# Refilling the operands of the down product one by one, on GpSimd's DMA queue

## The chip, the cores and the metric

One core of a Trainium2 chip. The metric is the device time of one execution in microseconds (us), as the median of several runs. All engine times below are from one profiled execution of the kernel.

## What is computed

The reference is one layer of a decoder (sparse attention beside retention, then a feed-forward block, then a gated embedding) on 1024 prompt tokens and 8 sample tokens. The change touches the feed-forward block alone:

```python
hn = rms_norm(h, n2)
h = h + (jax.nn.silu(hn @ wg) * (hn @ wu)) @ wd      # D_MODEL 1024, D_FF 2816
```

All of it is float32. The kernel writes each operand as a sum of a rounded high part and a low part (`split`), and each product as three matmuls (`mm3`: high by high, high by low, low by high).

## The kernel before

**Tiling.** The 1032 tokens are cut into two halves (`p` = 0, 1) of two quarters (CE = 258 tokens each); the features run on the partitions. `D_FF` is walked in NF = 11 slabs `f` of 256 features. Gate, up and down are computed by a fast two-by-two scheme: instead of eight block products, seven, numbered 1 to 7. Each has a weight operand (a sum or difference of blocks of the weights) and an activation operand `x1` to `x7` (the same of blocks of the activations). Gate and up use them in the order `FAST` = 1, 6, 5, 2, 7, 4, 3, down in the order `DOWN` = 1, 5, 6, 3, 2, 4, 7.

**Gate and up** (`gate_up`, L1840; `fast_product`, L1702). For each slab and each half the seven products of the gate, then of the up weights, run on TensorE. `run` (L1735) interleaves two of them: the last two products (4 and 3) of one come behind the first two (1 and 6) of the next. Their partial sums lie in a tile `wst` (2 buffers, L1713), and `up` and `finish` leave the seven operands of the down product in `act`, which SyncE's DMA queue stores to `act_d` in HBM (L1864), since the operands of all slabs don't fit on the chip.

**Down** (`down`, L1927). The 11 slabs are taken in three parts, `PARTS` = slabs 0 to 2, 3 to 6, 7 to 10. In each part, for four column groups `mp` of the down weights, and in each for both halves `p`, the seven products of `kt` matmul triples run (3 triples in part 0, else 4) and are added into the result `h` (L1944 a copy on ScalarE, L1946 an add on VectorE). A product's sum lies in one of seven banks of PSUM, which come free with these adds.

**Fetching the operands** (`act_fetch`, L1877). The seven operands `x1` to `x7` of a half have one buffer each (`xtile`, L1751), the same that gate and up used. For each operand `act_fetch` loads two slabs at a time (258 KB), or the third slab alone (129 KB), into a raw tile, and `split` (L150) makes of it the high part by a cast on ScalarE (L152) and the low part by a subtraction on VectorE (L142, by L153). So each half and part takes 14 loads, and both halves 28. The raw tiles lie in two rings: `st` with three buffers, and `wst`, the ring of the gate and up products, with two; three loads of five use `st`. In the program `act_fetch` of part 0 stands ahead of the first `down` of each half (L1982), that of the next part behind the last `down` of the half (L1985).

**What sets the order.** The kernel is written with a scheduler: it puts each engine's instructions in an order of its own at compile time, by readiness in its own model of time and by the order of the program, and adds the semaphores. An instruction may so stand far ahead of its place in the program, where its buffer and its data allow; but once the order is made, each engine and each DMA queue works strictly in order, and an instruction that waits holds up all behind it. SyncE's queue issues the loads of `act_fetch`, those of the weights (`fast_weights`, L1675, L1680, tiles `wu`) and, in part 2, those of the residual (`h_d`, L1965, tiles `st`).

Of the kernel before, what the change touches and what calls it, by code (L numbers as in the profile page):

```python
# [10 lines left out]
F32 = mybir.dt.float32  # L11
# [109 lines left out]
def hybrid_kernel(tc, I, C, O):  # L121
# [1577 lines left out]
            operand(n, place[n])  # L1699
        return w  # L1700

    def fast_product(w, x, kt, take):  # L1702


        ba, bb, bc = bank("s", NS), bank("m", 2), bank("t", NT)

        def prod(b, n, first=True):

            for k in range(kt):
                mm3(b[:, :CE], w[n][0][:, k], w[n][1][:, k], x[n][0][:, k], x[n][1][:, k], first and k == 0, k == kt - 1,  # L1710
                    skip_group_check=not first)

        st = tl(pdr, [128, 2, CE], "wst", bufs=2)  # L1713
        s, t1, u3 = st[:, 0], st[:, 1], tl(pdr, [128, CE], "wu3")
        prod(ba, 1)
        A.copy(s, ba[:, :CE])
        prod(bb, 6)
        add(V, t1, bb[:, :CE], s)
        yield
        prod(bc, 5)  # L1720
        prod(ba, 2, False)
        take(0, 0, ba[:, :CE], None)
        prod(bb, 7, False)
        add(V, u3, bb[:, :CE], s)
        take(1, 1, bc[:, :CE], u3)
        yield
        prod(bb, 4, False)
        take(1, 0, bb[:, :CE], s)
        prod(bc, 3, False)
        take(0, 1, bc[:, :CE], t1)  # L1730
        yield
# [3 lines left out]
    def run(product, then=None):  # L1735

        if product:
            next(product)
        if going:
            g, f = going.pop()  # L1740
            next(g)
            if f:
                f()
        if product:
            next(product)
            going.append((product, then))
# [93 lines left out]
    def gate_up(w, f):  # L1840
# [27 lines left out]
        w = fast_weights(half_rows(I["w_up"], f * 256), 4, FAST)  # L1868
        for p in range(2):
            act = tl(pf, [128, 8, CE], "act", bufs=2)  # L1870
            run(fast_product(w, xs[p], 4, partial(up, p, act)), partial(finish, p, act))

    PARTS = ((0, 3), (3, 4), (7, 4))

    staged = [0]

    def act_fetch(p, f0, kt):  # L1877
        for n in DOWN:
            full[p][n] = xtile(p, n)
            xs[p][n] = hi, lo = tuple(x[:, :kt] for x in full[p][n])  # L1880
            for a in range(0, kt, 2):
                b = min(a + 2, kt)
                staged[0] += 1
                raw = tl(pdr, [128, 2, CE], *(("st", F32, 3), ("wst", F32, 2))[staged[0] % 5 % 2])[:, :b - a]
                SY.dma_start(raw, act_d[f0 + a:f0 + b, p, :, n - 1, :].rearrange("f p c -> p f c"))
                split(V, hi[:, a:b], lo[:, a:b], raw)

    w = fast_weights(half_rows(I["w_gate"], 0), 4, FAST)
    for g in (norm2(3), combine(1)):
# [37 lines left out]
    def down(n, kt, mp, p, w):  # L1927
# [6 lines left out]
        def prod(b, m, tag=None, bufs=None):  # L1934
            first = tag is not None
            if first:
                banks[b] = bank(tag, bufs)[:, :CE]
            for k in range(kt):
                mm3(banks[b], w[m][0][:, k], w[m][1][:, k], x[m][0][:, k], x[m][1][:, k], first and k == 0, k == kt - 1,
                    skip_group_check=not first)  # L1940

        def onto(c, b, fresh):
            if n == 0 and fresh:
# [33 lines left out]
    for n, (f0, kt) in enumerate(PARTS):  # L1977
        for mp in range(4):
            w = fast_weights(lambda half: wdv[half, :, f0:f0 + kt, mp * 256:(mp + 1) * 256], kt, DOWN)
            for p in range(2):  # L1980
                if n + mp == 0:
                    act_fetch(p, f0, kt)  # L1982
                down(n, kt, mp, p, w)
                if mp == 3 and n < 2:
                    act_fetch(p, *PARTS[n + 1])  # L1985
                elif mp == 3:
                    h_parts(p, range(8))
                    p_parts(p)

# [103 lines left out]
```

## Time and profile before

| | |
|---|---|
| median of 3 runs (lowest to highest) | 2144.17 us (2142.01 to 2145.64) |
| the profiled execution: its own time, its span | 2140.78 us, 2139.0 us |
| granted TensorE clock, mean | 0.986 of full speed |
| TensorE (PE) busy | 2045.0 us, 96% of the span |
| VectorE (DVE) busy | 1370.5 us, 64% |
| ScalarE (ACT) busy | 843.5 us, 39% |
| GpSimd (POOL) busy | 690.6 us, 32% |

The span runs from the first to the last instruction. PE is TensorE's matmul, PEld its weight load, DVE VectorE, ACT ScalarE, POOL GpSimd, SP SyncE; a q behind the name means its queue or sequencer. L152 is line 152 of the kernel. A releaser ("<-") is what ended an idle time, inferred from the semaphores; idle time of an engine that is not the bound costs nothing by itself. Gate and up end and the down product starts near 1764 us; down ends near 1995 us.

### The profile page before, as it was taken

The numbers are of one execution on the slowest core, as the hardware profiler recorded it, in microseconds if no ns is written. First come the engines' busy times: TensorE is split into PE (matmuls) and PEld (weight loads), VectorE is DVE, ScalarE is ACT, GpSimd is POOL, SyncE is SP. The second block draws the span as 40 slices with busy tenths as digits, with TensorE's granted clock in tenths as the row PEclk, the third lists the DMA queues.
The fourth block names the chain that finished last, engine by engine and source line by source line (L and its number), as shares of the span: only waits on it lengthen the run. The fifth ranks groups of instructions, "written<-read, shape, count | busy, mean of one in ns | idle before, by whom it ended". The sixth has DMA issues, their size and how long they took to land.

```text
span 2139.0 us, 38497 instructions
## 1 busy us (share of the span) xinstructions
PE 2045.0 (96%) x14824; PEld 1895.3 (89%) x14824; DVE 1370.5 (64%) x3135; ACT 843.5 (39%) x2091; POOL 690.6 (32%) x891
## 2 busy tenths in 40 slices
PE   7999999979999999999999898999999999999998
PEld 6998998867788886679999798999999999999998
DVE  4335145357778889677665458766666676878632
ACT  3331222236565654554444334323323335542321
POOL 1235334277777765757673033000000000000100
PEclk9999999989999999999999998999999999999999
DMA  6322223244334343644541731233233244553221
GB/s 225 136 73 74 75 69 87 59 125 134 106 117 123 109 126 109 204 145 143 158 153 44 218 95 47 94 122 107 79 112 102 85 141 147 179 154 125 91 74 50
DMA packets 186032, 246.77 MB, mean 115 GB/s; under 512 B 17252, under 2 KB 155144, under 8 KB 185656
## 3 DMA queue, kind: packets, MB, share of 16 engines
q1 hardware_dynamic: 160760, 160.40, 24.4%
q0 software_dynamic: 25088, 83.90, 12.6%
q8 instruction: 117, 1.92, 0.4%
q14 instruction: 67, 0.55, 0.1%
HBM read 204.09 MB, written 44.34 MB: 116 GB/s over the span
## 4 chain that ended last, share of the span: by engine, by line
PE 53%; DVE 6%; DMA 4%; ACT 1%; issue 1%; POOL 0%; DVEq 0%; ACTq 0%; POOLq 0%; SPq 0%
PE m L944 8%; PE s L157 5%; PE s L159 5%; PE s L158 5%; PE m L157 4%; PE m L159 4%; PE m L158 4%; PE t L157 3%; PE t L159 3%; PE t L158 3%; PE t L1144 2%; DMA wst<-act_d 2%; DVE x L142 1%; PE o L1133 1%; PE s L1268 1%
## 5 line engine op out<-in xcount | busy, mean ns | idle before, releaser
L944 PE MATMUL m<-seg,w1h 128*128 128x256 f32 x1024 | 296.3, 396 | 0.8 <-DVE scl L1048 0.8
L157 PE MATMUL s<-x,wu 128*128 128x258 f32 x872 | 248.9, 286 | 5.3 <-ACT x L152 3.3
L158 PE MATMUL s<-x,wu 128*128 128x258 f32 x872 | 248.5, 285 | 1.0 <-DVE x L142 0.9
L159 PE MATMUL s<-x,wu 128*128 128x258 f32 x872 | 247.8, 284 | 0.5 <-DVE wu L142 0.5
L142 POOL TENSOR_TENSOR x<-h,x 128x516 fp32r<-128x516 f32 x4 | 5.7, 1415 | 676.9 <-ACT x L152 676.9
L157 PE MATMUL m<-x,wu 128*128 128x258 f32 x768 | 218.9, 286 | 2.6 <-DVE h L148 1.5
L158 PE MATMUL m<-x,wu 128*128 128x258 f32 x768 | 218.1, 284 | 2.5 <-DVE x L142 2.5
L159 PE MATMUL m<-x,wu 128*128 128x258 f32 x768 | 217.9, 284 | 0.0
L944 PEld LDWEIGHTS m<-seg,w1h 128*128 128x128 f32 x1024 | 173.9, 194 | 20.8 <-issue 8.9
L152 ACT CAST wu<-wu 128x512 fp32r<-128x512 f32 (+2 forms) x178 | 109.6, 626 | 193.4 <-DVE wu L142 119.1
L953 DVE STREAM_TRANSPOSE seg<-raw 128x1024 f32<-128x1024 f32 x128 | 158.6, 1240 | 37.5 <-PE m L944 29.9
L157 PEld LDWEIGHTS s<-x,wu 128*128 128x128 f32 x872 | 165.8, 190 | 6.3 <-ACT x L152 3.7
L158 PEld LDWEIGHTS s<-x,wu 128*128 128x128 f32 x872 | 166.5, 191 | 1.6 <-DVE x L142 1.4
L159 PEld LDWEIGHTS s<-x,wu 128*128 128x128 f32 x872 | 166.4, 191 | 0.7 <-DVE wu L142 0.7
L142 DVE TENSOR_TENSOR wu<-wu,wu 128x512 fp32r<-128x512 f32 (+2 forms) x178 | 126.6, 715 | 61.7 <-ACT wu L152 60.1
L157 PE MATMUL t<-x,wu 128*128 128x258 f32 x528 | 150.8, 286 | 7.3 <-DVE h L148 4.9
L290 PE MATMUL g<-wh,xnh 128*128 128x256 f32 (+3 forms) x504 | 148.9, 296 | 2.5 <-ACT xnh L340 2.3
L158 PE MATMUL t<-x,wu 128*128 128x258 f32 x528 | 149.6, 283 | 0.5 <-DVE x L142 0.4
L159 PE MATMUL t<-x,wu 128*128 128x258 f32 x528 | 149.4, 283 | 0.3 <-DVE wu L142 0.3
L157 PEld LDWEIGHTS m<-x,wu 128*128 128x128 f32 x768 | 146.1, 190 | 4.0 <-issue 1.7
L158 PEld LDWEIGHTS m<-x,wu 128*128 128x128 f32 x768 | 146.6, 191 | 2.7 <-DVE x L142 2.7
L854 POOL DMA_INDIRECT raw<-in_cache_cmp_v_dram,cix x128 | 126.6, 989 | 66.9 <-issue 28.5
(474 smaller groups left out, 5977.8 us busy)
## 6 DMA issues: line engine op xcount, KB each, us to landing
act_d<-act SPq DMA_DIRECT2D x22, 903.0 KB
wr<-in_w_in_dram SPq DMA_DIRECT2D x12, 1024.0 KB
wu<-in_w_gate_dram SPq DMA_DIRECT2D x22, 512.0 KB
wu<-in_w_up_dram SPq DMA_DIRECT2D x22, 512.0 KB
st<-act_d SPq DMA_DIRECT2D x42, 258.0 KB
wu<-in_w_down_dram SPq DMA_DIRECT2D x16, 512.0 KB
wst<-act_d SPq DMA_DIRECT2D x28, 258.0 KB
mr<-mix_d SPq DMA_DIRECT2D x16, 258.0 KB
```

Source lines behind the costliest of these rows:

```text
L142: eng.tensor_tensor(out=out, in0=a, in1=b, op=ALU.subtract)
L152: A.copy(hi, src)
L157: P.matmul(out, wh, xh, start=first, stop=False, **kw)
L158: P.matmul(out, wh, xl, start=False, stop=False, **kw)
L159: P.matmul(out, wl, xh, start=False, stop=last, **kw)
L290: P.matmul(pt[:r, :n], xh, wh[:, k, :n], start=k == 0, stop=False)
L854: G.indirect_dma_start(out=raws[n, par][:, x, :], out_offset=None, in_=crow[kv], in_offset=bass.IndirectOffsetOnAxis(ap=cix[:, par, col:co ...
L944: P.matmul(out, w[:, k, :], x[:, k // 2 % 2, :, k % 2, :], start=first and k == 0, stop=k == 7, skip_group_check=not first)
L953: V.transpose(t.rearrange("p k (x d) -> p k x d", x=4), raws[n, par][:, :, s2 * 256:(s2 + 1) * 256].rearrange("p x (k d) -> p k x d", k=8))
L1133: P.matmul(u.po[:, :256], st[2], ph[:, x, :], start=u.done == 0, stop=False)
L1144: P.transpose(pt[:, (x * 2 + r) * 128:(x * 2 + r + 1) * 128], src[:, r, c0:c0 + 128], ident)
L1268: P.matmul(pt[x * 64:(x + 1) * 64, :256], qzb[:, b, :], kt[:, x * 256:(x + 1) * 256], start=True, stop=True)
```

## The change

Each operand is fetched right behind the last product that reads it: part 0 from within the last up product of each half (a new argument `used` of `fast_product`), the later parts from within `down` of the last column group. The loads are issued by GpSimd's queue in place of SyncE's. In part 0 they all use the ring `st`; the later parts use `st` and `wst` as before. The arithmetic is the same.

```diff
-    def fast_product(w, x, kt, take):
+    def fast_product(w, x, kt, take, used=None):
...
             for k in range(kt):
                 mm3(b[:, :CE], w[n][0][:, k], w[n][1][:, k], x[n][0][:, k], x[n][1][:, k], first and k == 0, k == kt - 1,
                     skip_group_check=not first)
+            if used:
+                used(n)
...
-            run(fast_product(w, xs[p], 4, partial(up, p, act)), partial(finish, p, act))
+            run(fast_product(w, xs[p], 4, partial(up, p, act), partial(act_fetch, p, 0) if f == NF - 1 else None),
+                partial(finish, p, act))
...
-    def act_fetch(p, f0, kt):
-        for n in DOWN:
-            full[p][n] = xtile(p, n)
-            xs[p][n] = hi, lo = tuple(x[:, :kt] for x in full[p][n])
-            for a in range(0, kt, 2):
-                b = min(a + 2, kt)
-                staged[0] += 1
-                raw = tl(pdr, [128, 2, CE], *(("st", F32, 3), ("wst", F32, 2))[staged[0] % 5 % 2])[:, :b - a]
-                SY.dma_start(raw, act_d[f0 + a:f0 + b, p, :, n - 1, :].rearrange("f p c -> p f c"))
-                split(V, hi[:, a:b], lo[:, a:b], raw)
+    def act_fetch(p, part, n):
+
+        f0, kt = PARTS[part]
+        full[p][n] = xtile(p, n)
+        xs[p][n] = hi, lo = tuple(x[:, :kt] for x in full[p][n])
+        for a in range(0, kt, 2):
+            b = min(a + 2, kt)
+            staged[0] += 1
+            raw = tl(pdr, [128, 2, CE], *(("st", F32, 3), ("wst", F32, 2))[part and staged[0] % 5 % 2])[:, :b - a]
+            G.dma_start(raw, act_d[f0 + a:f0 + b, p, :, n - 1, :].rearrange("f p c -> p f c"))
+            split(V, hi[:, a:b], lo[:, a:b], raw)
...
                 mm3(banks[b], w[m][0][:, k], w[m][1][:, k], x[m][0][:, k], x[m][1][:, k], first and k == 0, k == kt - 1,
                     skip_group_check=not first)
+            if mp == 3 and n < 2:
+                act_fetch(p, n + 1, m)
...
-                if n + mp == 0:
-                    act_fetch(p, f0, kt)
                 down(n, kt, mp, p, w)
-                if mp == 3 and n < 2:
-                    act_fetch(p, *PARTS[n + 1])
-                elif mp == 3:
+                if mp == 3 and n == 2:
                     h_parts(p, range(8))
                     p_parts(p)
```

## Rows read from the trace of the kernel before

**Rows 1.** The page: engines over the span; GpSimd's only elementwise work around the down product.
```profile
PE 2045.0 (96%) x14824; PEld 1895.3 (89%) x14824; DVE 1370.5 (64%) x3135; ACT 843.5 (39%) x2091; POOL 690.6 (32%) x891
...
L142 POOL TENSOR_TENSOR x<-h,x 128x516 fp32r<-128x516 f32 x4 | 5.7, 1415 | 676.9 <-ACT x L152 676.9
```

**Rows 2.** Busy time in five stretches: bounds and length, engines, PEclk, DMA share, GB/s.
```profile
1735.00:1764.00 29.00, 27.09 (x225) 26.82 (x223) 21.18 (x47) 12.09 (x27) 0.00 (x0) 1.00 0.53 156
1764.00:1797.00 33.00, 29.86 (x222) 28.38 (x221) 25.27 (x56) 17.83 (x42) 0.00 (x0) 0.95 0.61 186
1816.00:1850.00 34.00, 29.37 (x240) 28.77 (x239) 29.73 (x54) 22.88 (x45) 0.00 (x0) 1.00 0.81 241
1850.00:1899.00 49.00, 49.00 (x410) 49.00 (x410) 35.31 (x70) 12.66 (x22) 0.00 (x0) 1.00 0.25 78
1899.00:1935.00 36.00, 32.51 (x261) 31.32 (x260) 31.80 (x62) 20.69 (x36) 0.00 (x0) 1.00 0.75 222
```

**Rows 3.** Timeline of TensorE: matmuls behind idle time (start, duration, [idle <-releaser]).
```profile
1760.27 0.51 PE L157 MATMUL s<-x,wu 128*128 128x258 f32 x2 [1.91 <-ACT x L152]
...
1832.38 0.39 PE L157 MATMUL t<-x,wu 128*128 128x258 f32 x1 [2.70 <-DVE h L148]
...
1839.71 0.39 PE L157 MATMUL t<-x,wu 128*128 128x258 f32 x1 [0.68 <-ACT wu L152]
...
1933.96 0.36 PE L157 MATMUL t<-x,wu 128*128 128x258 f32 x1 [2.04 <-DVE h L148]
```

**Rows 4.** Timeline of VectorE ahead of the matmul at 1832.38 us.
```profile
1831.29 0.69 DVE L142 TENSOR_TENSOR x<-wst,x 128x516 fp32r<-128x516 f32 x1 [1.48 <-ACT x L152]
1831.91 0.42 DVE L148 TENSOR_TENSOR h<-t,h 128x258 f32<-128x258 f32 x1
```

**Rows 5.** Timeline of ScalarE: casts of operands of part 1, and of a weight.
```profile
1816.97 1.15 ACT L152 CAST x<-st 128x516 fp32r<-128x516 f32 x2
...
1819.07 0.63 ACT L152 CAST x<-wst 128x516 fp32r<-128x516 f32 x1
...
1822.75 0.63 ACT L152 CAST x<-st 128x516 fp32r<-128x516 f32 x1 [1.35 <-DMA st<-act_d]
...
1932.13 0.62 ACT L152 CAST wu<-wu 128x512 fp32r<-128x512 f32 x1 [5.41 <-DMA wu<-in_w_down_dram]
```

**Rows 6.** The chain that ended last, in order of time: start us, us, what.
```profile
1754.58 4.99 DMA wst<-act_d
...
1821.47 3.19 DMA wst<-act_d
...
1826.08 4.54 DMA wst<-act_d
```

**Rows 7.** Timeline of SyncE's queue: DMA issues (start, time spent, tile, count).
```profile
1438.91 1.29 SPq L1885 DMA_DIRECT2D st<-act_d  x3
...
1742.18 0.37 SPq L1885 DMA_DIRECT2D st<-act_d  x1
...
1748.24 0.33 SPq L1885 DMA_DIRECT2D st<-act_d  x1
...
1787.74 2.47 SPq L1885 DMA_DIRECT2D wst<-act_d  x2
...
1819.93 0.97 SPq L1885 DMA_DIRECT2D st<-act_d  x2
...
1846.68 0.47 SPq L1885 DMA_DIRECT2D wst<-act_d  x1
...
1923.63 2.02 SPq L1965 DMA_DIRECT2D st<-h_d  x2
1925.70 1.61 SPq L1680 DMA_DIRECT2D wu<-in_w_down_dram  x2
```

**Rows 8.** GpSimd's gathers by source line L854: duration ns min/median/max; landing.
```profile
L854 POOL DMA_INDIRECT raw<-in_cache_cmp_k_dram,cix x128: 942/958/1978, 428.2 to 741.3; - x128
...
DMA to landing us min/median/max: 3.2/3.6/5.1
```

## The prediction

> **What bounds the kernel now.** First the engines over the whole span: TensorE is busy for 2045.0 of 2139.0 us, every other engine for less than two thirds [rows 1]. So a change can only pay where TensorE stands still, and the second view is the busy time by stretches around the down product. The reader should compare each length with TensorE's column: between the bursts of fetching it is full (49.00 of 49.00 us, 410 matmuls, so 0.12 us each), and in each burst it is not [rows 2]. The holes are 1.91 us in 1735 to 1764 and 3.14 us in 1764 to 1797 (part 0), 4.63 us in 1816 to 1850 (part 1), 3.49 us in 1899 to 1935 (part 2): 13.2 us. In the second stretch the granted clock is also only 0.95 in the mean [rows 2]; between the levels of 1.2 and 2.4 GHz that is a tenth of the stretch at the lower one, and 5% of 33 us, 1.65 us, of work lost. All that this change can reach is thus 14.8 us, 0.7% of the time.
>
> Third, the timeline of TensorE tells whom it waited for [rows 3]. At 1760.27 it waited 1.91 us for the cast of an operand of part 0; at 1832.38, 2.70 us for an add that frees its bank; at 1839.71, 0.68 us for a weight's cast; at 1933.96, 2.04 us for another add. These four are 7.33 of the 13.2 us; the others are shorter. The add that freed the bank at 1832.38 was not late by itself: it stands on VectorE behind the subtraction of a fetched operand, which waited 1.48 us for its cast [rows 4], and that for a load issued at 1826.08 that took 4.54 us to land [rows 6]. So **a late load stops engines that work in order, and these stop TensorE**. Where the loads of part 0 are late the reason is the ring: a load into `wst` goes out only at 1754.58 [rows 6], though three loads into `st` went out at 1438.91 [rows 7], since the up products still hold `wst`.
>
> **The change, part by part.**
>
> *Fetching behind the last product.* This sounds like the main thing, and I count it at nothing in parts 1 and 2, for the trace shows that it is so already: five casts of part 1's operands run from 1816.97 to 1819.70 without a wait for a DMA [rows 5], inside the last column group of part 0, so their loads had landed ahead and they ran as soon as the buffers came free. The sixth waits, for a load [rows 5]. What limits the burst after that is the slots: 5 raw tiles, each going through load, cast and subtraction.
>
> *Part 0: ring and order.* The load that waited for `wst` is gone, and with it the hole of 1.91 us: **-1.9 us**; bounds 0 (another operand is late in its place) and -1.9 - 3.1 - 1.65 = -6.7 us (all of part 0's loss). Against that, 28 loads now pass through 3 slots, not 5. Three still go out early. The slot refilled at 1742.18 is refilled at 1748.24, three loads on, so a slot turns in 6.06 us here [rows 7]; the quickest turn in the chain is 1821.47 to 1826.08, 4.61 us [rows 6]. With 25 loads left, 25 / 3 turns are 38 to 50 us from 1742: the end lies at 1780 to 1793. Before, the slots were being refilled for part 1 at 1787.74 to 1790.21 [rows 7], so part 0 was through by 1790. I take the longer turn, since it is of this very stretch: 3 us later than before.
>
> *GpSimd's queue.* No load of this shape from this queue is in the trace. Its nearest rows are the gathers, 128 rows of 2 KB: 0.958 us of GpSimd (0.942 to 1.978) and 3.6 us to landing (3.2 to 5.1) [rows 8]. SyncE's loads of 258 KB took 3.19 and 4.54 us in the chain [rows 6]. Taking 3.6 against a middle of 3.3, a turn gets 0.3 us longer: 8.3 turns in part 0, 28 / 5 = 5.6 in each later part, so 2.5, 1.7 and 1.7 us of lateness. With part 0's 3 us that makes 8.9 us. TensorE lost 4.63 of 34 and 3.49 of 36 us in such bursts [rows 2], 0.12 us per us; so the lateness costs **+1.0 us**. Bounds: 0 (the next column group's seven products, 7 x 12 x 0.12 = 10 us, cover it all) and the slow rival below. GpSimd does nothing in these stretches [rows 2]; behind the loads on its queue stand only four subtractions of 1.4 us at the end of part 2 [rows 1], when the last fetch is long over.
>
> *SyncE's queue without the fetches.* At 1932.13 the cast of a weight has waited 5.41 us for its load [rows 5], which went out at 1925.70, right behind two loads of the residual that took SyncE 2.02 us [rows 7]; these stood behind the fetches. TensorE's 2.04 us at 1933.96 end that chain. With the fetches on another queue the weights can go out when their buffers are free: **-2.0 us**, and likewise the 0.68 us at 1839.71: **-0.7 us**. Bounds: 0 (they wait for the buffer `wu` or stay behind the residual) and -2.7. SyncE is spared three times 28 issues, each of 0.33 to 0.47 us [rows 7], some 30 us, which cost nothing in themselves.
>
> *Order on VectorE and ScalarE.* A fetched operand now stands ahead of the adds of its own product in the program. Each add can come later by one subtraction (0.69 us [rows 4]), against seven banks of 1.4 us: nothing, at worst 0.7 us per burst.
>
> **Sum:** -1.9 - 2.0 - 0.7 + 1.0 = -3.6 us. The profiled execution has a span of 2139.0 us and a time of 2140.78, 1.8 us around it; it would come to 2137.2. The median of the runs is 2144.17, 3.4 us above that execution, and the forecast is set on the median: **2140.5 us**, 0.17% less.
>
> **A rule against it.** A weight's load at 1925.70 goes out at once when the two before it are issued [rows 7]. The Trainium skill, page "DMA: Bandwidth & Descriptors", section "Issuing engines are not separate DMA queues", says that transfers from several engines run on the same DMA engines, and that issuing from a second one saves only issue time. By that alone the weights' 2.7 us would stay, and the sum would be -0.9 us, 2143.3. The row speaks for a wait in the queue, which is not issue time, so I keep the 2.7.
>
> **Rivals.**
>
> *The holes close (2130 to 2136, say 2133).* The scheduler gets the operands of part 0 five us sooner for half 0 (they no longer share `wst`), TensorE meets no hole above 2 us, the clock stays at its upper level, and the late adds go because loads from the other queue land evenly. For it: all holes hang on the fetches [rows 2, 3]. Against: DMA is busy for 0.81 and 0.75 of the bursts [rows 2] and the bytes are the same. Price: three quarters of 14.8, -11 us.
>
> *GpSimd becomes the pace of the bursts (2149 to 2177, say 2156): slower.* In the burst of part 1 SyncE issued 28 loads (14 for each half) from 1819.93 to 1846.68 [rows 7]: 0.96 us each. GpSimd's gather costs 0.958 [rows 8], just as much; these loads have 256 runs, not 128. So the point from which it decides is 0.96 us a load. At 1.4 us the two later bursts end 28 x 0.44 = 12 us later each; half of that covered, TensorE loses 12 us: 2156. At 1.98, the longest gather, they end 28 us later, less 10 of cover, twice: +36, with what part 0 keeps 2177. For it: the doubled runs. Against: that the median gather is so close to the shortest, 0.958 to 0.942, which looks like a fixed cost. The longest gather, 1.978 us, shows that something can double the price, and VectorE is busy for 0.88 of the two later bursts [rows 2]. The Trainium skill ("SBUF — State Buffer", section "Who interferes with whom") says that VectorE in a two-port mode locks GpSimd out of SBUF, and counts an operation on two tensors, which VectorE runs here, not among these modes; by it these loads would stay near the median.
>
> *Nothing moves (2144).* The fetches were hoisted already, the queue makes no odds, and the ring of three takes what the ring of five lost.
>
> **How the numbers follow.** The small gain has 0.44 (2136 to 2144), the closed holes 0.24, the slow queue 0.26, nothing 0.06. About 0.2%, 4.3 us, is what a measurement of this kernel can tell from no change: below 2139.9 is faster, above 2148.5 slower. Of the small gain's 0.44, 0.14 lies below 2139.9; with 0.24 faster is 0.38. Same is 0.30 of it and nearly all of the 0.06: 0.36. Slower is the slow queue, 0.26. The range goes from 2130, where all reachable loss is gone (14.8 us less is 2129.4), to 2156, the middle of the slow queue; it leaves out half of that case and a little below, 0.16. The likeliest case's own range is 2136 to 2144.
>
> **What would show it.** Right: no idle time for a cast near 1760 us; the weight's load of part 2 issued clearly before 1925 and no hole of 2 us after it; GpSimd's loads near 1.0 us each; bursts of 28 to 30 us. Wrong: GpSimd busy end to end through the bursts at over 1.2 us a load, with waits of ScalarE for `act_d` loads grown, and TensorE behind adds; or a hole of over 5 us before 1797, from the ring of three.

## The result, and the profile after

The changed kernel takes **2162.49 us** (median; 2159.95 to 2164.46), beside 2144.9 us for the kernel before on the same chip (2142.01 to 2148.67). The ratio is **1.0089**, with a 95% interval of 1.0071 to 1.0107: slower by 0.9%, some 18 us, where 0.17% less was forecast. It lies outside the range. The profiled execution of the changed kernel took 2163.55 us with a span of 2161.8, against 2140.78 and 2139.0.

The page's first line, to be held against [rows 1]: TensorE's busy time is 5.0 us longer for the same 14824 matmuls, and GpSimd has 84 instructions more.

```profile
PE 2050.0 (95%) x14824; PEld 1901.5 (88%) x14824; DVE 1370.0 (63%) x3135; ACT 844.0 (39%) x2091; POOL 747.8 (35%) x975
```

To find the place, take the stage of the down product: from the first issue of a down weight to the first issue of a weight of the gated embedding behind it. It begins at 1735.4 us in the kernel before and at 1735.3 in the changed one, and lasts 242.8 and 265.9 us: **23.1 us more**, which is the whole difference of the two spans (22.8). Windows over that stage, first before, then after (columns as in [rows 2]):

```profile
1735.40:1978.20 242.80, 229.63 (x1862) 226.10 (x1861) 190.85 (x385) 105.24 (x207) 0.00 (x0) 0.99 0.50 152
```

```profile
1735.30:2001.20 265.90, 236.12 (x1862) 233.07 (x1861) 191.23 (x385) 105.69 (x206) 56.20 (x81) 0.95 0.45 139
```

The same 1862 matmuls: TensorE stands still for 29.8 us where it stood for 13.2, so 16.6 us, and is busy for 6.5 us longer, since the granted clock fell from 0.99 to 0.95 in the mean. GpSimd is busy for 56.2 us of the stage. The stretches of [rows 2] again, for the changed kernel:

```profile
1735.00:1764.00 29.00, 24.55 (x202) 24.14 (x201) 20.17 (x46) 12.77 (x29) 9.66 (x16) 0.98 0.45 130
1764.00:1797.00 33.00, 22.98 (x147) 22.41 (x148) 18.76 (x42) 12.49 (x29) 9.73 (x15) 0.76 0.65 201
1816.00:1850.00 34.00, 30.63 (x250) 30.00 (x250) 20.77 (x39) 18.61 (x39) 11.56 (x16) 1.00 0.54 170
1850.00:1899.00 49.00, 44.02 (x353) 43.60 (x352) 39.47 (x77) 18.78 (x32) 8.66 (x12) 0.97 0.39 121
1899.00:1935.00 36.00, 32.97 (x273) 32.58 (x272) 24.83 (x49) 14.87 (x25) 10.89 (x16) 1.00 0.43 128
```

The worst is 1764 to 1797: 147 matmuls in 33 us, where there were 222, at a clock of 0.76, so half of it at the lower level. By TensorE's waits over the stage (columns: who waited and for whom, us in all, times, the longest):

```profile
PE s L157 <- ACT h L1950: 10.0, 1, 10.0
PE t L157 <- ACT wu L152: 6.2, 2, 4.2
PE t L157 <- DVE h L148: 4.6, 4, 2.0
PE m L157 <- DVE wu L148: 4.5, 2, 4.3
```

The longest is a hole of 9.96 us that ends at 1785.63 with a copy into `h` on ScalarE (now L1950). TensorE's timeline shows the hole, and ScalarE's ahead of it shows why the copy was late:

```profile
1785.63 0.58 PE L157 MATMUL s<-x,wu 128*128 128x258 f32 x1 [9.96 <-ACT h L1950]
```

```profile
1771.05 0.41 ACT L152 CAST x<-st 128x258 fp32r<-128x258 f32 x1 [1.97 <-DMA st<-act_d]
...
1778.78 0.62 ACT L152 CAST x<-st 128x516 fp32r<-128x516 f32 x1 [0.51 <-DMA st<-act_d]
1781.97 0.41 ACT L152 CAST x<-st 128x258 fp32r<-128x258 f32 x1 [2.56 <-DMA st<-act_d]
...
1785.21 0.64 ACT L1950 COPY h<-s 128x258 f32<-128x258 f32 x2
```

Operand casts that stand ahead of the copy wait for one load after another; the copy is behind them in order, and the banks that it frees are what TensorE needs. The loads themselves, by source line, before and after (duration ns min/median/max, first to last start), with what waited for them:

```profile
L1885 SPq DMA_DIRECT2D st<-act_d x50: 319/360/830, 1438.9 to 1922.4; - x50
...
ACT x L152: 24.4, 28
```

```profile
L1889 POOL DMA_DIRECT2D st<-act_d x62: 560/722/846, 1399.1 to 1943.1; - x62
L1889 POOL DMA_DIRECT2D wst<-act_d x22: 722/722/727, 1758.5 to 1942.4; - x22
...
DVE x L142: 438.2, 40
...
ACT x L152: 51.2, 50
DMA to landing us min/median/max: 2.3/3.4/8.4
```

A load costs GpSimd 0.72 us (0.56 for the 129 KB ones), twice SyncE's 0.36, but its issues alone don't set the pace: the 28 loads of the burst of part 1 keep it busy for 20.2 of 33.2 us, and in between it stands idle, mostly until VectorE has freed a raw slot. ScalarE's casts wait 51.2 us for loads in all, not 24.4.

**One turn of a slot.** In the kernel before, the subtraction that frees a `wst` slot starts at 1831.29 and takes 0.69 us [rows 4], and SyncE has the next load on its way 0.04 us later:

```profile
1832.02 0.36 SPq L1885 DMA_DIRECT2D wst<-act_d  x1
```

In the changed kernel such a subtraction ends at 1837.81, and GpSimd starts 0.30 us later and takes 0.72 us (VectorE's timeline, then GpSimd's):

```profile
1837.13 0.68 DVE L142 TENSOR_TENSOR x<-wst,x 128x516 fp32r<-128x516 f32 x1
```

```profile
1838.11 0.72 POOL L1889 DMA_DIRECT2D wst<-act_d  x1 [0.21 <-issue]
```

Over the 51 loads of the two later bursts, from the end of the subtraction that frees a slot to the end of that of the load that takes it, the median turn is 4.89 us before and 5.84 after: the pick-up is 0.27 us longer in the median (0.03 to 0.30), the time from issue to landing 0.27 (3.35 to 3.62 us, the longer issue within it). The rest lies in a few loads that land late. By the semaphore updates in the trace the five that leave from 1842.40 to 1847.22, beside a pair of weights that SyncE sends at 1842.1 and 1843.2, take 6.5 to 8.4 us to land, the other 23 of this burst 3.0 to 4.5; in the kernel before the pair leaves behind 24 of the burst's 28 loads. So in the mean of the 46 turns that lie within a burst, 4.97 us before and 6.09 after, the pick-up is 0.39 us longer and the landing 0.81, while cast and subtraction take no longer. The burst of part 1 (28 loads: 23 of part 1, and the first five of part 2) goes from 26.75 us [rows 7] to 32.5 us, 1831.18 to 1863.68.

### The profile page after: what moved, and what is told of

It is laid out like the page before. It is cut to its first block, busy times and chain, and to the rows that moved or that the text cites. A ratio compares the mean times of both kernels' runs of the same rounds, so it can differ in the third digit from the quotient of the medians.

```text
span 2161.8 us, 38526 instructions
## 1 busy us (share of the span) xinstructions
PE 2050.0 (95%) x14824; PEld 1901.5 (88%) x14824; DVE 1370.0 (63%) x3135; ACT 844.0 (39%) x2091; POOL 747.8 (35%) x975
## 5 line engine op out<-in xcount | busy, mean ns | idle before, releaser
L1889 POOL DMA_DIRECT2D st<-act_d x62 | 42.5, 686 | 552.8 <-DVE x L142 433.9
L157 PE MATMUL t<-x,wu 128*128 128x258 f32 x528 | 152.3, 289 | 10.9 <-ACT wu L152 6.2
L158 PE MATMUL t<-x,wu 128*128 128x258 f32 x528 | 151.2, 286 | 0.3 <-DVE x L142 0.3
L159 PE MATMUL t<-x,wu 128*128 128x258 f32 x528 | 150.9, 286 | 0.0
L854 POOL DMA_INDIRECT raw<-in_cache_cmp_v_dram,cix x128 | 126.7, 990 | 66.9 <-issue 28.4
```

Source lines behind the costliest of these rows:

```text
L157: P.matmul(out, wh, xh, start=first, stop=False, **kw)
L158: P.matmul(out, wh, xl, start=False, stop=False, **kw)
L159: P.matmul(out, wl, xh, start=False, stop=last, **kw)
L854: G.indirect_dma_start(out=raws[n, par][:, x, :], out_offset=None, in_=crow[kv], in_offset=bass.IndirectOffsetOnAxis(ap=cix[:, par, col:co ...
L1889: G.dma_start(raw, act_d[f0 + a:f0 + b, p, :, n - 1, :].rearrange("f p c -> p f c"))
```

## The experiments

The ratios are to the kernel before on the same chip, with 95% intervals; 0.1% is 2.1 us. Stage and parts are of the one profiled execution of each kernel and worked out from issues on the queues: part 0 from the first down weight to the first refill of the burst of part 1, part 1 from there to the first refill of the burst of part 2, part 2 to the end of the stage; a burst is from its first to its last refill; idle is TensorE's time between matmuls in the stage. All in us.

| kernel | ratio | stage | part 0 | part 1 | part 2 | burst 1 | burst 2 | idle |
|---|---|---|---|---|---|---|---|---|
| before | 1 | 242.8 | 84.6 | 81.2 | 77.0 | 26.8 | 21.2 | 13.2 |
| after | 1.0089 (1.0071 to 1.0107) | 265.9 | 95.9 | 87.2 | 82.8 | 32.5 | 24.8 | 29.8 |
| q_alone | 1.0086 (1.0065 to 1.0108) | 257.8 | 92.0 | 86.8 | 78.9 | 31.5 | 24.7 | 21.3 |
| all_but_q | 1.0037 (1.0023 to 1.0051) | 248.1 | 85.8 | 85.1 | 77.1 | 27.6 | 21.2 | 16.1 |
| p0_alone | 1.0012 (0.9999 to 1.0025) | 243.7 | 85.7 | 81.4 | 76.6 | 26.5 | 22.2 | 15.3 |
| p12_alone | 1.0009 (0.9996 to 1.0022) | 246.8 | 84.6 | 84.7 | 77.4 | 28.1 | 21.5 | 15.0 |
| g_old_order | 1.0111 (1.0092 to 1.0129) | 257.4 | 91.9 | 86.6 | 78.9 | 31.5 | 24.1 | 21.5 |
| sy_new_order | 1.0047 (1.0030 to 1.0064) | 247.5 | 88.6 | 82.4 | 76.5 | 28.2 | 22.3 | 18.0 |
| w_on_g | 1.0056 (1.0039 to 1.0072) | 251.6 | 84.7 | 85.8 | 81.0 | 30.1 | 25.6 | 16.7 |
| g_part0 | 1.0036 (1.0023 to 1.0050) | 249.4 | 90.5 | 81.4 | 77.5 | 26.4 | 23.0 | 16.2 |
| one_queue_g | 1.0067 (1.0050 to 1.0084) | 256.9 | 92.7 | 85.9 | 78.4 | 30.7 | 23.9 | 19.7 |
| g_w_held | 1.0058 (1.0041 to 1.0075) | 262.3 | 92.2 | 88.4 | 81.8 | 28.9 | 24.0 | 22.8 |
| ring7 | 1.0025 (1.0014 to 1.0035) | 249.3 | 79.3 | 88.3 | 81.7 | 23.1 | 17.5 | 18.6 |
| g_ring7 | 1.0073 (1.0056 to 1.0089) | 263.1 | 86.5 | 91.5 | 85.2 | 26.8 | 20.0 | 31.3 |
| sy_h_first | 0.9996 (0.9986 to 1.0005) | 243.0 | 84.0 | 82.1 | 76.8 | 29.2 | 22.8 | 10.9 |
| g_h_first | 1.0076 (1.0063 to 1.0089) | 257.4 | 91.9 | 87.4 | 78.1 | 34.6 | 24.2 | 21.1 |
| after_h_first | 1.0069 (1.0056 to 1.0082) | 259.7 | 91.5 | 86.1 | 82.2 | 32.7 | 25.4 | 26.0 |
| g_all_first | 1.0083 (1.0068 to 1.0099) | 261.9 | 93.1 | 86.9 | 82.0 | 35.0 | 27.6 | 23.0 |
| sy_all_first | 1.0069 (1.0054 to 1.0083) | 258.9 | 87.9 | 91.6 | 79.4 | 37.5 | 22.9 | 26.4 |
| g_w_first | 1.0094 (1.0080 to 1.0109) | 263.6 | 91.9 | 88.5 | 83.2 | 36.7 | 28.8 | 25.1 |

In the two kernels with seven slots, burst 2 has 21 refills; in all others it has 23. One profiled execution differs from the next by some us, so a stage is read together with its ratio.

### Which part of the change

**q_alone**: the queue, and nothing else.

```diff
-                SY.dma_start(raw, act_d[f0 + a:f0 + b, p, :, n - 1, :].rearrange("f p c -> p f c"))
+                G.dma_start(raw, act_d[f0 + a:f0 + b, p, :, n - 1, :].rearrange("f p c -> p f c"))
```

> The kernel before with its operand loads on GpSimd's queue, and nothing else changed. Theory A (most of the 17 us comes from part 0, refetched through three slots of one ring from inside the last up products; the queue adds what the two later bursts lost): 4 to 8 us slower than before, the hole of part 0 no longer than before (5 us of TensorE idle in 1735 to 1797). Theory B (the queue is the cause, through a longer turn of every slot): 13 to 20 us slower. Theory C (the later parts' place in the program is the cause there): within 3 us of before.

**all_but_q**: the changed kernel, fetches on SyncE.

```diff
-            G.dma_start(raw, act_d[f0 + a:f0 + b, p, :, n - 1, :].rearrange("f p c -> p f c"))
+            SY.dma_start(raw, act_d[f0 + a:f0 + b, p, :, n - 1, :].rearrange("f p c -> p f c"))
```

> The changed kernel with its operand loads on SyncE's queue. Theory A: 10 to 16 us slower than before, so some 4 to 8 us better than the changed kernel. Theory B: within 5 us of before. Theory C: as slow as the changed kernel, 15 to 20 us slower than before.

**p0_alone**: all_but_q with the new place and the ring `st` for part 0 only.

```diff
-            if mp == 3 and n < 2:
-                act_fetch(p, n + 1, m)
...
-                if mp == 3 and n == 2:
+                if mp == 3 and n < 2:
+                    for m in DOWN:
+                        act_fetch(p, n + 1, m)
+                if mp == 3 and n == 2:
```

> The kernel before with part 0 alone changed: fetched from inside the last up products, through the ring st only, on SyncE's queue. Theory A: 10 to 16 us slower than before, with holes of 4 us and of 10 us before 1797. Theory B: within 4 us of before, since the slots turn as fast as they did. Theory C: as theory A.

**p12_alone**: all_but_q with the new place for parts 1 and 2 only.

```diff
-            run(fast_product(w, xs[p], 4, partial(up, p, act), partial(act_fetch, p, 0) if f == NF - 1 else None),
+            run(fast_product(w, xs[p], 4, partial(up, p, act), None),
...
-            raw = tl(pdr, [128, 2, CE], *(("st", F32, 3), ("wst", F32, 2))[part and staged[0] % 5 % 2])[:, :b - a]
+            raw = tl(pdr, [128, 2, CE], *(("st", F32, 3), ("wst", F32, 2))[staged[0] % 5 % 2])[:, :b - a]
...
+                if n + mp == 0:
+                    for m in DOWN:
+                        act_fetch(p, 0, m)
                 down(n, kt, mp, p, w)
```

> The kernel before with the place of the later two parts' fetches alone changed, on SyncE's queue. Theories A and B: within 3 us of before, since those fetches ran as soon as their buffers came free already. Theory C: 4 to 8 us slower, with the casts of weights late behind the operands' casts.

**What follows.** The queue alone costs 0.86%, nearly all that the change costs; everything else together costs 0.37%, and its two halves, each alone, can't be told from nothing. Theory B's numbers held in three of the four; all_but_q, some 8 us slower (5 to 11), lies above B's 5 us and below the 10 to 16 of A. Of A's numbers only that of p12_alone held, of C's none. The parts don't simply add (0.86 and 0.37 against 0.89), and each of these kernels also has an order of its own from the scheduler, which is not told apart from the edit here.

### The queue at run time, or the order it was compiled to

The scheduler models a fetch on GpSimd differently from one on SyncE, so q_alone also has another order on TensorE, VectorE and ScalarE. In the next kernels that order is held, by edges that make no instruction wait (`names` is the order of one engine or queue in the stage):

```diff
+        for a, b in zip(names, names[1:]):
+            tc.add_manual_dep(tc.nc.find_inst_by_name(b), a,
+                              mybir.DependencyInfo(mybir.DependencyClass.NoSync, mybir.DependencyReason.DATA), reason="order")
```

**g_old_order**: q_alone with the order of the kernel before.

> The kernel before with the fetches on GpSimd's queue, and every engine's instructions held in the order that they have in the kernel before (the fetches on GpSimd in the order that they had on SyncE). q_alone changed two things: the queue at run time, and with it the order that the scheduler gave to VectorE, ScalarE and TensorE at compile time. Theory T (slot turn: GpSimd takes up the freed slot 0.3 us later and issues 0.35 us slower, so operands come late): the whole loss stays, +12 to +20 us against the kernel before. Theory O (order: operand casts compiled ahead of the copies of the h sums hold TensorE up): the loss goes, 0 to +4 us. Theory C (two queues move operands and weights at once and land each other late): +10 to +16 us, with landings of 5 us and more.

**sy_new_order**: the kernel before with the order of q_alone.

> The kernel before, fetches on SyncE, but every engine's instructions in the order that the scheduler gave them when the fetches were on GpSimd (the order of q_alone). Theory T: 0 to +3 us, since the slot turn is SyncE's. Theory O: +10 to +18 us, the loss of q_alone without its queue. Theory C: 0 to +3 us.

**w_on_g**: fetches on SyncE, order of before, the down weights on GpSimd.

```diff
-            SY.dma_start(t, src(half))
+            (G if order is DOWN else SY).dma_start(t, src(half))
```

> The kernel before, its order on VectorE, ScalarE and TensorE held, fetches on SyncE, and the 24 loads of down weights on GpSimd's queue instead: two queues, but no GpSimd in the operands' slot turn. Theory T: within 3 us of the kernel before. Theory O: within 3 us. Theory C: +6 to +14 us, with operand landings of 5 to 7 us where a weight load is issued beside them.

**g_part0**: as g_old_order, for part 0 only.

```diff
-                SY.dma_start(raw, act_d[f0 + a:f0 + b, p, :, n - 1, :].rearrange("f p c -> p f c"))
+                (SY if f0 else G).dma_start(raw, act_d[f0 + a:f0 + b, p, :, n - 1, :].rearrange("f p c -> p f c"))
```

> As g_old_order, but only the 28 loads of part 0 go through GpSimd; the 56 of parts 1 and 2 stay on SyncE. Theory T: by the number of loads that a part waits for, a third to a half of g_old_order's loss (+5 to +9 us if that is +15), all of it before the burst of part 1. Theory O: 0 to +3 us. Theory C: the share of part 0 alone, where SyncE's stores of act_d and weights run beside the fetches: +5 to +10 us.

**What follows.** With its order held the queue still costs 1.11% (24 us, above the 12 to 20 of theory T), so the loss is not a matter of the compiled order: theory O falls. Order isn't free either: q_alone's, on SyncE, costs 0.47%, some 10 us, where O had 10 to 18 and both others at most 3. In g_part0 the loss stands just where the loads go through GpSimd, as T and C both had it: part 0 is 5.9 us longer, parts 1 and 2 are nearly as before (81.4 and 77.5 against 81.2 and 77.0). But w_on_g, whose operands never see GpSimd, loses 0.56%, some 12 us, in parts 1 and 2, as theory C alone had it, so something about two queues costs too. GpSimd's timeline shows a weight pair that leaves at 1836.29 and 1837.50, in the midst of the burst that began at 1827.3; the kernel before sent it at 1843.40, behind 24 of the 28 loads (w_on_g, then the kernel before):

```profile
1836.29 0.75 POOL L1680 DMA_DIRECT2D wu<-in_w_down_dram  x1 [15.00 <-PE s L159]
1837.50 0.75 POOL L1680 DMA_DIRECT2D wu<-in_w_down_dram  x1 [0.46 <-PE m L159]
```

```profile
1843.40 1.01 SPq L1680 DMA_DIRECT2D wu<-in_w_down_dram  x2
```

A megabyte of weights then moves beside the operands: the five operand loads from 1836.4 to 1841.5 land only 6.2 to 8.3 us after their issue, the other 23 after 2.7 to 4.9, and the burst takes 30.1 us. On one queue the pair keeps its place behind those 24 loads, since the queue is in order. That the weights come late because GpSimd issues them is a rival that no run takes apart; in part 0, whose weights it issues too, nothing is lost (84.7 against 84.6 us).

### GpSimd's own price, or two queues

**one_queue_g**: order of before, and all that SyncE issued among the fetches on GpSimd, in SyncE's order.

```diff
-            SY.dma_start(t, src(half))
+            (G if order is DOWN else SY).dma_start(t, src(half))
...
-            SY.dma_start(act_d[f, p], act[:, 0:7])
+            (G if f == NF - 1 else SY).dma_start(act_d[f, p], act[:, 0:7])
...
-                SY.dma_start(raw, act_d[f0 + a:f0 + b, p, :, n - 1, :].rearrange("f p c -> p f c"))
+                G.dma_start(raw, act_d[f0 + a:f0 + b, p, :, n - 1, :].rearrange("f p c -> p f c"))
```

> The kernel before with its order held on TensorE, VectorE and ScalarE, and GpSimd's queue in SyncE's place for everything that SyncE issued among the fetches: the 84 fetches, the 24 loads of down weights and the two last stores of act_d, in SyncE's order. One queue again, and only GpSimd's own price is left. Theory T (the slot turn through GpSimd is 0.3 us later at the pick-up and 0.35 us at the issue): the loss stays, +12 to +22 us, part 0 +6 or more. Theory C (two queues move operands beside weights and stores, which one queue had kept apart): 0 to +6 us, and the bursts of parts 1 and 2 within 1.5 us of the 26.8 and 21.2 us of the kernel before. Half and half: +7 to +12 us.

**g_w_held**: g_old_order with three weight loads held until a subtraction `behind` is done.

```diff
+        tc.add_manual_dep(tc.nc.find_inst_by_name(f"I-{load}"), f"I-{behind}",
+                          mybir.DependencyInfo(mybir.DependencyClass.Sync, mybir.DependencyReason.DATA), reason="hold")
```

> As g_old_order (fetches on GpSimd, old order), but three loads of down weights on SyncE (the second of part 0, the pair that fell into the burst of part 1) wait for the VectorE subtraction that freed the slot of the fetch ahead of them in the kernel before, so that they leave as late as they did on SyncE's single queue. Theory C: the stretch from the first refill of part 1 to that of part 2 falls from 86.6 us to 81 to 83 us (81.2 in the kernel before), the burst of part 1 from 31.5 to under 29 us. Theory T: the stretch stays within 1.5 us of 86.6, the burst within 1 us of 31.5, and the total at +17 to +25 us.

**ring7** and **g_ring7**: seven raw slots, fetches on SyncE and on GpSimd.

```diff
-        return tl(pwt, [128, T], "wu", F32R, bufs=12) if p is None else tl(p, [128, 1024], "wx", F32R, bufs=4)
+        return tl(pwt, [128, T], "wu", F32R, bufs=11) if p is None else tl(p, [128, 1024], "wx", F32R, bufs=5)
...
-                raw = tl(pdr, [128, 2, CE], *(("st", F32, 3), ("wst", F32, 2))[staged[0] % 5 % 2])[:, :b - a]
+                raw = tl(pdr, [128, 2, CE], *(("st", F32, 5), ("wst", F32, 2))[staged[0] % 7 in (1, 4)])[:, :b - a]
```

> The kernel before on SyncE with seven raw slots in place of five (five of one tag, two of the other; one weight tile less, 11 of 12, pays for them, and one more staging tile in the w_out stage). Theory T (bursts are bound by slots times turn): at 7 slots and a turn of 5.2 us the bound is 0.74 us a load, so the burst of part 1 falls from 26.8 to 21 to 24 us, the stage by 3 to 8 us, the total by as much less what the missing weight tile costs (0 to 4 us). Theory C: 0 to -3 us, since the DMA engines, not the slots, set the pace while anything else moves.

> The change's queue with seven raw slots (as ring7, fetches on GpSimd, place and the rest as before). Theory T: the longer turn is covered by two more slots (6.0 us over 7 is 0.86 us a load, below the 0.96 of the kernel before), so it is within 4 us of ring7 and within 4 us of the kernel before. Theory C: weights still move during the bursts, so it stays 8 us or more above ring7.

**What follows.** one_queue_g has a single queue again and still loses 0.67%, some 14 us, where theory T had 12 to 22 and C at most 6; its stage, 256.9 us, and its bursts, 30.7 and 23.9, are those of g_old_order within 1 us. So GpSimd's own price, on the operands' slots and here on the weights too, is enough for a loss: theory T. Its timeline shows GpSimd waiting for VectorE as in the changed kernel, the weight pair now again behind 24 of the operands' loads:

```profile
1857.45 0.72 POOL L1885 DMA_DIRECT2D st<-act_d  x1 [0.40 <-DVE x L142]
1858.17 1.49 POOL L1680 DMA_DIRECT2D wu<-in_w_down_dram  x2
1859.65 0.71 POOL L1885 DMA_DIRECT2D wst<-act_d  x1
```

How much two queues add is not settled. By the ratios it is 0.67% against 1.11%, whose intervals don't overlap, though the kernels ran on two chips; by the profiled stages it is nothing, but the profiled execution of g_old_order (2161.39 us) was the shortest of its four, 9.7 us below their median, so that its stage shows too little of its loss. The mean turn within the later bursts speaks for a share of each: 4.97 us before, 5.56 in one_queue_g, 5.82 in w_on_g, 5.85 in g_old_order. g_w_held is mixed. Holding the weights back shortens the burst to 28.9 us, as C said, and the loss to 0.58%, some 12 us, where T had 17 to 25; but the stretch grows to 88.4, which neither theory had, in an execution 4.8 us longer than its median. ring7 shortens the burst to 23.1 us, as T said, and part 0 by 5.3 us; yet it is slower, which neither theory had. TensorE's waits now end mostly with casts and subtractions of weights (12.8 of 18.6 us, where it was 1.0 of 13.2):

```profile
PE m L159 <- DVE wu L142: 5.7, 1, 5.7
PE s L157 <- ACT h L1944: 4.6, 1, 4.6
PE s L157 <- ACT wu L152: 3.6, 1, 3.6
```

Whether the missing weight tile or the new order that the scheduler made for these kernels does that was not tested. And g_ring7's burst is 26.8 us, that of the kernel before, but it is 0.48% slower than ring7, some 10 us, where T had at most 4 and C 8 or more. So T's cure by slots misses in both, and the length of a burst is not the whole price. No run made SyncE's turn longer by itself: that the longer turn is what costs is the likeliest reading of these runs, not shown alone.

### How a late load reaches TensorE

In g_old_order eleven of the 14 operands of part 1 are through their last subtraction 8 to 22 us ahead of their first product, and the other three 2 to 5 us. TensorE's waits in that part end not with operands but with additions into `h` (4.3 us) and a weight's cast (1.7), which stand behind the operands' casts and subtractions. So such operations were moved ahead of them. One of the moves from g_old_order to g_h_first, in VectorE's order (other operations between these left out):

```diff
 x_3847<-wst_20564,x_3847
+h_19661<-s_20656,h_19661
 x_3847<-st_20568,x_3847
 x_3850<-st_20573,x_3850
 x_3850<-wst_20577,x_3850
 x_3853<-st_20582,x_3853
 x_3853<-wst_20586,x_3853
 x_3856<-st_20591,x_3856
-h_19661<-s_20656,h_19661
```

**sy_h_first**, **g_h_first**, **after_h_first**: additions and copies into `h` first, in the kernel before, in g_old_order and in the changed kernel.

> The kernel before (fetches on SyncE), its order held but for one thing: on VectorE and ScalarE each addition or copy of a product into the h sums stands where its product was ready in the profile of before, ahead of the operand subtractions and casts that wait for later loads. Theory H (a late load reaches TensorE through the h additions that stand behind its cast and subtraction on the in-order engines, since they hold the PSUM banks): the 4.6 and 2.7 us of holes in the bursts of parts 1 and 2 go, -3 to -8 us. Theory D (TensorE waits for the operands themselves): 0 within 2 us.

> The same edit on g_old_order (fetches on GpSimd, order of before), from its own profile. Theory H: parts 1 and 2 give back what they lost, 4 to 8 us of its +14.6 us of stage, so +6 to +11 us against the kernel before. Theory D: the loss stays, stage at +13 us or more, total at +14 us or more.

> The same edit on the changed kernel, from its own profile (its h additions were up to 12 us behind their products). Theory H: its stage of 265.9 us falls by 6 to 14 us, the total to +4 to +13 us against the kernel before. Theory D: within 3 us of the changed kernel, +15 to +22 us.

**g_all_first**, **sy_all_first**: then all weight operations ahead as well.

> g_h_first (fetches on GpSimd, h additions ahead of the operand subtractions) with the casts, additions and subtractions of the next weights moved ahead as well, by up to 6 us, to where the profile of g_h_first has their inputs ready. Only the operands' own casts and subtractions then wait for loads. Theory W (the loss goes through whatever stands behind the waiting operands on the in-order engines; with the h additions out of the way it was a weight subtraction that ended a hole of 7.1 us): the hole goes, the stage falls from 257.4 to 248 to 253 us, the total to +5 to +10 us. Rival (VectorE and ScalarE have too much work in the burst, whatever the order): stage within 2 us of 257.4, total as g_h_first, +14 to +18 us.

> The same edit on sy_h_first, with SyncE's fetches as before. Theory W: its holes of 1.7, 1.8 and 2.7 us that ended with weight casts or subtractions go, -3 to -7 us against the kernel before, and it beats both kernels. Rival: within 2 us of the kernel before.

**g_w_first**: from g_h_first, only those of the first weights of parts 1 and 2. One move, as above:

```diff
+wu_20640<-wu_20626,wu_20640
 x_3840<-wst_20481,x_3840
 x_3840<-st_20485,x_3840
 x_3847<-wst_20564,x_3847
...
-wu_20640<-wu_20626,wu_20640
```

> g_h_first with only those weight casts, additions and subtractions moved ahead of the operand work that belong to the first weights of parts 1 and 2: their loads landed long before the burst (g_all_first moved also a cast of later weights, whose own load comes behind the burst, and ScalarE waited for it). Theory W: the 7.1 us hole of the burst of part 1 and the 4.2 us one of part 2, which ended with such operations, go; the stage falls from 257.4 to 246 to 252 us, the total to +5 to +10 us against the kernel before. Rival (GpSimd's slot turn sets the pace whatever the order): stage within 2 us of 257.4, total at +13 us or more.

**What follows.** In g_h_first the waits for `h` are gone, as theory H wanted, but the stage is still 257.4 us and the total some 16 us up, as D had it: the largest hole now ends with a weight subtraction. sy_h_first shows the same on SyncE: its waits for `h` fall from 8.4 to 1.6 us, those for weights grow from 1.0 to 6.8, and the time stays. after_h_first, some 15 us up, lies between the two theories. TensorE's waits over the stage of g_h_first:

```profile
PE m L159 <- DVE wu L142: 7.1, 1, 7.1
PE t L157 <- ACT x L152: 6.3, 2, 3.5
PE t L157 <- ACT wu L152: 4.5, 2, 4.2
```

VectorE's timeline shows that subtraction behind operands that come late:

```profile
1842.68 0.70 DVE L142 TENSOR_TENSOR x<-st,x 128x516 fp32r<-128x516 f32 x1 [2.09 <-ACT x L152]
1844.80 0.70 DVE L142 TENSOR_TENSOR x<-wst,x 128x516 fp32r<-128x516 f32 x1 [1.42 <-ACT x L152]
1845.41 0.69 DVE L142 TENSOR_TENSOR wu<-s,wu 128x512 fp32r<-128x512 f32 x1
```

With these weights ahead too (g_w_first) the operands themselves are late, and the bursts take 36.7 and 28.8 us, since each slot now waits longer for its subtraction (median turn 6.81 us, in g_h_first 5.85):

```profile
PE s L157 <- ACT x L152: 6.5, 3, 3.0
PE t L157 <- ACT x L152: 5.9, 2, 3.0
PE t L157 <- ACT wu L152: 5.7, 2, 3.4
```

Theory W falls. Its rival's total (13 us or more) held, its stage did not (263.6 us for 257.4). The wait goes from one kind of work to the next and the sum stays: h additions, weights and operands share two engines in order, and no order that was tried gave the loss back. By the ratios the first edit gave a little: g_h_first 1.0076 against 1.0111 for g_old_order, on other chips; after_h_first 1.0069 against 1.0089, whose intervals overlap. g_all_first and sy_all_first say something else: a cast of later weights had been moved ahead of its own load, and ScalarE stood there for it (sy_all_first, ScalarE, then TensorE):

```profile
1858.50 0.62 ACT L152 CAST wu<-wu 128x512 fp32r<-128x512 f32 x1 [6.92 <-DMA wu<-in_w_down_dram]
```

```profile
1862.02 0.58 PE L159 MATMUL m<-x,wu 128*128 128x258 f32 x1 [10.25 <-DVE wu L142]
```

The same work, place and queue as the kernel before cost 0.69% more, by order alone. No kernel here beats the kernel before; sy_h_first equals it.

## Why the prediction was wrong

**The step that failed is "GpSimd's queue"**: +1.0 us in the sum, about +18 in the run with the queue alone (0.86%), +15.0 in its profiled stage. Its two factors:
- *The turn.* Taken as 0.3 us longer, from landings alone. In the two later bursts the median turn measured 4.89 us before and 5.90 in q_alone: the pick-up behind VectorE costs 0.27 us more, the time from issue to landing 0.35 (its longer issue included), and on top come the loads that leave beside a pair of weights (in q_alone those from 1848.0 to 1851.3 land after 6.3 to 7.1 us). The usual landing was about right, though the middle of 3.3 us taken for SyncE stands in none of the rows named beside it; the pick-up and the weights beside the loads were not in the sum. q_alone's bursts are 4.7 and 3.4 us longer, where 1.7 each was said; the last load of part 0 leaves 47.4 us behind its first within the stage, for 43.1 before, so 4.3 us later, where 2.5 was said.
- *What TensorE pays.* 0.12 us per us of lateness, read from TensorE's idle share in a burst [rows 2]. That is a mean, not a slope: it told how much was lost at that length of burst and nothing of one more microsecond. In g_part0 part 0 became 5.9 us longer for a stretch of fetching that was 6.0 us longer (49.1 against 43.1 us, first to last load of part 0 within the stage), and parts 1 and 2 of q_alone 5.6 and 1.9 us longer for the bursts named above. Nor is it a fixed price: sy_h_first's bursts are 2.4 and 1.6 us longer, and its time is the same. The stated cover, ten us of the next column group, was not there, since that group's weights and the `h` additions stand in the same queues of ScalarE and VectorE. The clock came on top: 6.5 of the changed kernel's 23.1 us are longer matmuls at the lower granted clock.

**The rival "GpSimd becomes the pace"** gave 2156 us, nearest to the truth, but by luck, for its reason didn't hold. Its point was 0.96 us a load; the load takes 0.72. The burst of part 1 goes at 1.16 us a load, and GpSimd is idle for 13.0 of its 33.2 us. The loss came without a full queue. (The 28 loads were read as 14 for each half; they are 23 of part 1 and five of part 2, which changes nothing in that sum.)

**"SyncE's queue without the fetches"** (-2.7 us) gave nothing back. The weights of part 2 whose load went out at 1925.70 [rows 7] leave no earlier: they still stand behind loads of the residual, now on a queue without fetches:

```profile
1943.11 6.85 SPq L1971 DMA_DIRECT2D st<-h_d  x3
1950.06 0.93 SPq L1680 DMA_DIRECT2D wu<-in_w_down_dram  x2
```

That is 31.7 us behind the first refill of part 2 (1918.35), where it was 24.5 before: the residual goes through the raw ring `st` too, whose slots the operands hold. The bound "stay behind the residual" was the right end. And the holes that end with a weight's cast grew from 0.7 us to 6.2. Ahead of the one of 4.20 us at 1855.22 the cast waited not for its load but for its turn on ScalarE:

```profile
1848.95 0.62 ACT L152 CAST x<-st 128x516 fp32r<-128x516 f32 x1 [2.76 <-DMA st<-act_d]
...
1851.51 0.62 ACT L152 CAST x<-wst 128x516 fp32r<-128x516 f32 x1 [1.67 <-DMA wst<-act_d]
...
1855.07 0.62 ACT L152 CAST wu<-wu 128x512 fp32r<-128x512 f32 x1
```

In part 1 a weight pair does leave earlier than before, 10.9 us into the burst where it was 23.5, and the loads beside it are the five that land late; w_on_g shows the same with SyncE's loads. So what the sum took for a gain, weights that go out when their buffers are free, made operands late in part 1.

**"A rule against it".** The Trainium skill, page "DMA: Bandwidth & Descriptors", section "Issuing engines are not separate DMA queues", gave the better number for this term: by it the 2.7 us were not to be had, and they were not. The part of it that says that such transfers run on the same DMA engines fits the loads that land late beside the weights; that a second queue also moves a wait in the queue, as the prediction held against it, is so in part 1, to the operands' cost. The other page quoted, "SBUF — State Buffer", section "Who interferes with whom", agrees with the trace: the loads stay at their median (722 ns, at most 846) though VectorE is busy beside them.

**"Part 0: ring and order"** (-1.9 us, bounds 0 and -6.7): p0_alone measured +0.12% (-0.01 to +0.25), its stage +0.9 us. The hole of 1.91 us at 1760 is gone, as said; one of 6.05 us at a copy into `h` stands in its place, so the bound at zero was the right end. The lateness counted for the ring of three was wrong: in p0_alone the last load of part 0 leaves 35.8 us behind the first within the stage, for 43.1 before, so 7.3 us sooner, not 3 later, and TensorE gained nothing by it. The longest of TensorE's waits in p0_alone:

```profile
PE s L157 <- ACT h L1948: 6.0, 1, 6.0
```

This is the "hole of over 5 us before 1797" that was named as a sign of error, and in the changed kernel, with the fetches on GpSimd, it is 9.96 us.

**"Fetching behind the last product"** at nothing: right within what can be told (p12_alone +0.09%, -0.04 to +0.22), though its profiled part 1 is 3.5 us longer. **"Order on VectorE and ScalarE"** at nothing was wrong in kind: only the change's own reordering was looked at, not that the scheduler makes another order when the queue changes. That order, on SyncE, costs 0.47%.

What stays open: why no reordering gave more of it back, how much of the loss the second queue adds beside GpSimd's price, and whether the same longer turn on SyncE would cost as much.

## What to carry to other kernels

Where a ring of slots feeds a burst, count the whole turn, from the instruction that frees a slot to the one that frees it again, pick-up and issue included: here the turn was a microsecond longer through a queue that was busy for only three fifths of a burst. A mean of idle time over work is no price of lateness; where engines work in order and everything that feeds TensorE shares them, let a later load cost up to its full length in the range, and take a cover for free only if it runs on other engines. A single queue also keeps transfers apart in time, so before moving some to another, look at what will then move beside them.

## What the runs showed of the hardware

GpSimd takes up a freed slot 0.30 us behind VectorE, SyncE 0.03 (medians of the two later bursts, after and before). A plain load costs GpSimd 0.56 us for 129 KB, 0.72 for 258 KB and 0.75 for 512 KB, so hardly more with the bytes, and less than its gather of 128 rows (0.942 at least, [rows 8]). From issue to landing a GpSimd load of 258 KB takes 3.62 us in the median, SyncE's 3.35; the longer issue lies within these, so that once on its way it is no slower. Beside a pair of 512 KB weights from the other queue five loads in a row took 6.5 to 8.4 us on GpSimd's queue (the changed kernel) and 6.2 to 8.3 on SyncE's (w_on_g); in the kernel before, behind such a pair on the same queue, the last two loads of the burst took 6.4.
